# A fused pooling-mixer kernel: first operands in smaller pieces, weights in 4 KB rows, the second fold by passes, the first product by halves

## The chip, the cores and the metric

The kernel runs on one core of one Trainium2 chip. The metric is the device time of one execution in microseconds; of the kernel before there are three runs, 907.3, 907.58 and 908.1, and the profile of one execution.

## The reference, cut to what matters

With DEPTH = 1 only mixer 0 runs. `x` is 4096 frames by 1024 channels, all in float32:

```python
def pool_mixer(h, in_w, group_w, group_b, scale, out_w):
    u, gate = jnp.split(h @ in_w, 2, axis=-1)
    ug = u.reshape(b, s, POOL_GROUPS, POOL_GROUP_DIM)
    pooled = jnp.stack([trailing_mean(ug[:, :, g], w) for g, w in enumerate(POOL_WINDOWS)], axis=2) - ug
    mixed = jnp.einsum('bsgc,gcd->bsgd', pooled, group_w) + group_b
    y = mixed.reshape(b, s, POOL_WIDTH) * scale * jax.nn.silu(gate)
    return y @ out_w
...
    normed = rms_norm(h, norm_w[i])
    h = h + pool_mixer(normed, ...)
return rms_norm(h, final_norm_w)
```

The group map of each of the four groups (256 by 256) is linear and the pooling acts along frames alone, so the map can be multiplied into the first half of `in_w` ahead of time. The kernel does this itself at its start; it is called the fold.

## The kernel before, in words

**The whole.** After the fold, the input product is done for four blocks of 1024 frames, each as seven products of a Strassen-like scheme (P1 to P7, in the order P1, P2, P7, P6, P5, P4, P3); all four blocks go through it for the gate side (steps "a"), then through it for the folded side (steps "b"), and eight blocks of 512 frames go through the output product (steps "o"). A float32 product is made of three passes: each operand is split into a high part (rounded to the type that the profile shows as fp32r) and a low part (the rest), and high by high, high by low and low by high are added up in a PSUM bank (`mm3`, L814). Splitting is one copy on ScalarE for the high part and one subtraction on VectorE for the low part (`split`).

**The opening.** Only this part is touched. It runs from the start to about 50 us, and TensorE's work in it stands in this order:

1. eight matmuls on a constant (L1702) that need no data;
2. fold 1 and fold 2, in plain float32 (`fold`, L466): 8 matmuls each, which the trace shows as 16 records each;
3. fold 3 and fold 4 by passes, 24 matmuls each, on split operands;
4. fold 5, fold 6, fold 7 and fold 8 in plain float32 again, 16 records each; in the middle of fold 6 stand eight small matmuls (L532, `spread_rs`) that spread the first rows' normalization factors `hl` over the partitions;
5. the first product P1 of the first block (L814, 48 matmuls), then P2, in which eight more `spread_rs` matmuls stand behind the second group of six.

Each fold reads one block of `wut` (512 KB, the transposed first half of `in_w`) and a set of two group maps `gw` (512 KB; set 0 for folds 1 to 4, set 1 for folds 5 to 8). The blocks are numbered here like the folds that read them: block 1 is `ru[0, 0]`, block 2 `ru[0, 4]`, block 3 `ru[0, 2]`, block 4 `ru[0, 6]`, block 5 `ru[1, 0]`, block 6 `ru[1, 4]`, block 7 `ru[1, 2]`, block 8 `ru[1, 6]`. A fold writes two banks; ScalarE or VectorE carries them out with the norm weights as factors.

**What sets the order.** All loads of the opening but two are issued by the sync engine (SP) in program order, and they use eight semaphores in turn, so a load is issued when the load eight places before it has landed. The order on the queue is: set 0 and block 1 (1 MB in four transfers of 256 KB, one of them issued by ScalarE), blocks 2 to 4, three pieces of `x` rows, set 1, block 5, and so on. The gate weights `g0` (two loads of 512 KB out of `in_w`, for P1's weights) stand on either side of block 8. In HBM the group maps lie in rows of 1 KB for one partition, `wut` and the gate half of `in_w` in rows of 2 KB, `x` and `xt` in rows of 4 KB. VectorE, ScalarE and TensorE run their lists in the order that the tile scheduler gave them.

**P1.** `product_in` runs the 48 matmuls of P1 bank by bank (`by_bank`): for each of four banks first half 0 of the contraction, then half 1. Half h needs the operand `op` that is split from `xs[0]["11"][h]` and the weights `w[P1][h]`. Its four results are copied to other banks between its groups (`copy_first`).

Of the kernel before, what the change touches and what calls it, by code (L numbers as in the profile page):

```python
# [15 lines left out]
P = 128  # L16
D = 1024
S = 4096
H = 512
# [67 lines left out]
def kernel(  # L87
# [5 lines left out]
    wut: bass.AP,  # L93
    group_w: bass.AP,
    cols: bass.AP,
    inv_count: bass.AP,
# [327 lines left out]

    def load_group_w(q, halves=(0, 1), g=None):
        if g is None:
            g = take("p (t c) -> p t c", early, t=4)
        for j in halves:
            c = slice(2 * j, 2 * j + 2)
            sync.dma_start(  # L430
                out=g[:, c, :], in_=group_w[2 * q + j].rearrange("(t p) c -> p t c", p=P)
            )
        return g

    def load_wut(q, k, queues=(sync,)):
        r = take("p (k t c) -> p k t c", early5, k=2, t=4)
        by = 2 // len(queues)
        for n, queue in enumerate(queues):
            kk = slice(n * by, (n + 1) * by)
            queue.dma_start(  # L440
                out=r[:, kk],
                in_=wut[q, k + n * by : k + (n + 1) * by].rearrange("k p t c -> p k t c"),
            )
        return r

    def split_early(place, u, pattern, **sizes):

        flat = place.rearrange("p s a b -> p s (a b)")
        split(flat, u.rearrange("p a b -> p (a b)" if len(u.shape) == 3 else "p k t c -> p (k t c)"))
        return [flat[:, j].rearrange(pattern, **sizes) for j in range(2)]  # L450

    def fold(q, k, g, r, ps2, pool=None, on_vector=False, midway=None):
# [22 lines left out]
        o = take(pool=pool)  # L475
        for kk in range(2):
            if on_vector and kk == 0:
                with tc.issue_after(roots[0][1]):
                    vector.tensor_scalar(
                        out=o[:, kk], in0=ps2[kk], scalar1=norm_c[k + kk], scalar2=None,  # L480
                        op0=ALU.mult,
                    )
            else:
                dst, src = o[:, kk], ps2[kk]
                if by_passes:
                    dst = dst.rearrange("p (j s a) -> p j s a", j=2, s=2)
                    src = src.rearrange("p (j a s) -> p j s a", j=2, s=2)
                scalar.activation(dst, src, AF.Copy, scale=norm_c[k + kk])
# [1003 lines left out]
    def run(n, between=None, behind=None, seeds=4):  # L1492
# [4 lines left out]
        if kind == "o":  # L1497
            product_out(i, split_up.pop(n), sets, n == len(steps) - 1)
            evict_o(b, i, sets)
        else:  # L1500
            q = 0 if kind == "a" else 1
            if inner_in(q, b, i):
                us, parts = xs[b]["2"], []
                at["split"] += 1

                def next_half():
                    parts.append(split_half(us[len(parts)]))

                product_seven(split_up.pop(n), sets["v"], next_half, next_half)
                if b == NB - 1:  # L1510
                    give_kept(*places_in)
                split_up[n + 1] = parts
            else:
                product_in(i, split_up.pop(n), sets, i == P1, between, behind)
            if "second" in seven:
                seven.pop("second")()
            evict_in(b, q, i, sets, seeds)
            if "third" in seven:
                seven.pop("third")()
            if inner_in(q, b, i):  # L1520
                for u in xs[b].pop("2"):
                    give(u)
# [177 lines left out]
    warm = nc.const_aps.tensor(1.0, [P, H], mybir.dt.bfloat16)  # L1700
    for c in range(8):
        nc.tensor.matmul(  # L1702
# [10 lines left out]
    for j in range(3):  # L1713
        load_row(0, 0, j)
    gw[1] = load_group_w(1, (0,))
# [4 lines left out]
    load_group_w(1, (1,), gw[1])  # L1720
# [30 lines left out]
    for j in range(4):  # L1751
        load_row(0, 1, j, early if j < 3 else None)
    g1 = [load_rows(in_w, 4 + 2 * h, D) for h in range(2)]
    load(2)
    load(3)

    for h in range(2):
        sub(v0[h], v1[h], v0[h])
        copy(w[P7][h][:, 0], v0[h])

# [292 lines left out]
```

## Time and profile before

| | |
|---|---|
| runs | 907.3, 907.58, 908.1 us (median 907.58) |
| the profiled execution | span 905.6 us from first to last instruction; the median of the runs is 2.0 us more, which is what lies around a span |
| instructions | 12443 |
| TensorE busy | 895.4 us, 99% of the span |
| VectorE, ScalarE, GpSimd busy | 737.0, 519.2, 152.2 us |
| DMA | 209.60 MB, mean 231 GB/s |

How it is read: PE is TensorE's matmul, DVE VectorE, ACT ScalarE, POOL GpSimd, SP the sync engine; SPq and ACTq are their queues' issues. Matmuls are pipelined, so a record is longer than the distance to the next one: in a row of n merged records the share of one is the row's time over n. In the page's digit rows each digit is a busy share in tenths. In the issue rows the last number is the time from issue to landing.

### The profile page before, as it was taken

How to read it: one execution, taken by the hardware profiler on the slowest of the kernel's cores; microseconds unless marked ns; L12 is line 12 of the kernel's file. 1: busy time of each engine (PE TensorE's matmuls, PEld its weight loads, DVE VectorE, ACT ScalarE, POOL GpSimd, SP SyncE). 2: the span in 40 equal slices, each digit the busy share in tenths (PEclk: the TensorE clock that was granted, in tenths of full speed). 3: DMA queues.
4: the chain of work that ended last, by engine and by line, in shares of the span. 5: the costliest groups of instructions: out<-in, count | busy, mean ns of one | idle time of the engine just before them, and what ended most of it. 6: DMA issues, size and time to landing. Idle time of an engine off the chain costs nothing.

```text
span 905.6 us, 12443 instructions
## 1 busy us (share of the span) xinstructions
PE 895.4 (99%) x4554; PEld 792.2 (87%) x4554; DVE 737.0 (81%) x910; ACT 519.2 (57%) x848; POOL 152.2 (17%) x250
## 2 busy tenths in 40 slices
PE   9999999999999999999999999999999999999996
PEld 7888888888888888889889888988889899998995
DVE  3899896984996996995485499698898788888798
ACT  7869547446445467446345654744557466565464
POOL 0030110110111000010100011021233343342330
PEclk9999999999999999999999999999999999999999
DMA  9989778678769475854245386699573855945953
GB/s 342 401 316 322 260 279 320 215 296 284 269 251 369 171 260 203 313 195 170 90 140 185 140 302 232 233 330 306 152 213 81 221 171 150 238 149 131 266 176 116
DMA packets 78620, 209.60 MB, mean 231 GB/s; under 512 B 7392, under 2 KB 25184, under 8 KB 77792
## 3 DMA queue, kind: packets, MB, share of 16 engines
q1 hardware_dynamic: 57872, 143.77, 45.7%
q0 software_dynamic: 19968, 63.98, 22.7%
q10 hardware_dynamic: 720, 1.06, 0.3%
q8 instruction: 35, 0.57, 0.3%
q14 instruction: 25, 0.20, 0.1%
HBM read 133.28 MB, written 75.51 MB: 231 GB/s over the span
## 4 chain that ended last, share of the span: by engine, by line
PE 88%; DVE 5%; DMA 3%; ACT 2%; issue 2%; POOL 0%; DVEq 0%; ACTq 0%; POOLq 0%; SPq 0%
PE bank L814 76%; PE bank L956 5%; PE bank L760 3%; PE bank L466 3%; DVE vt L79 2%; DVE op L79 2%; DVE st L79 1%; DMA vt<-yd 1%; DMA st<-wvd 1%; ACT vt L79 1%; DMA early<-in_group_w 0%; ACT st L79 0%; ACT op L79 0%; DMA out<-vt 0%; DVE columns L79 0%
## 5 line engine op out<-in xcount | busy, mean ns | idle before, releaser
L814 PE MATMUL bank<-op,w 128*128 128x512 f32 x2544 | 551.2, 379 | 1.5 <-ACT st L79 1.0
L814 PEld LDWEIGHTS bank<-op,w 128*128 128x128 f32 x2544 | 480.2, 189 | 70.9 <-ACT st L79 1.8
L814 PE MATMUL bank<-w,op 128*128 128x512 f32 (+1 forms) x1044 | 230.5, 377 | 0.0
L814 PEld LDWEIGHTS bank<-w,op 128*128 128x128 f32 x1044 | 192.3, 189 | 25.0
L79 DVE TENSOR_TENSOR op<-st,op 128x1024 fp32r<-128x1024 f32 x119 | 144.9, 1223 | 55.7 <-ACT op L79 55.4
L79 ACT ACTIVATE op<-st 128x1024 fp32r<-128x1024 f32 x119 | 124.8, 1052 | 81.6 <-PE bank L814 32.3
L79 ACT ACTIVATE op<-vt 128x1024 fp32r<-128x1024 f32 x66 | 69.4, 1053 | 70.0 <-DVE vt L79 41.7
L79 DVE TENSOR_TENSOR op<-vt,op 128x1024 fp32r<-128x1024 f32 x66 | 79.8, 1222 | 22.2 <-ACT op L79 22.1
L79 ACT ACTIVATE vt<-bank 128x512 f32<-128x512 f32 (+1 forms) x124 | 68.7, 577 | 46.0 <-PE bank L814 38.3
L79 DVE TENSOR_TENSOR st<-st,st 128x1024 f32<-128x1024 f32 (+2 forms) x49 | 54.8, 1134 | 30.4 <-ACT st L79 16.7
L79 ACT ACTIVATE bank<-bank 128x512 f32<-128x512 f32 (+1 forms) x84 | 41.1, 489 | 51.4 <-PE bank L814 38.6
L79 POOL COPY vt<-tails 128x32 f32<-128x32 f32 x14 | 17.5, 1257 | 271.7 <-DVE inner L79 106.8
L79 DVE TENSOR_TENSOR vt<-bank,vt 128x512 f32<-128x512 f32 (+1 forms) x92 | 52.9, 603 | 6.2 <-PE bank L956 4.6
L79 ACT ACTIVATE st<-bank 128x512 f32<-128x512 f32 (+1 forms) x60 | 34.2, 586 | 35.6 <-PE bank L814 25.0
L79 ACT ACTIVATE st<-st 128x1024 f32<-128x1024 f32 (+1 forms) x37 | 38.9, 1056 | 21.7 <-DVE st L79 19.7
L79 DVE TENSOR_TENSOR st<-bank,st 128x512 f32<-128x512 f32 (+1 forms) x70 | 42.6, 627 | 4.7 <-PE bank L956 2.5
L79 POOL DMA_DIRECT2D sd<-st x45 | 24.0, 533 | 125.7 <-DVE st L79 77.7
L956 PEld LDWEIGHTS bank<-w,op 128*128 128x128 f32 x312 | 40.4, 191 | 1.7
L956 PE MATMUL bank<-w,op 128*128 128x256 f32 x312 | 41.1, 275 | 0.0
L79 DVE TENSOR_TENSOR st<-st,vt 128x1024 f32<-128x1024 f32 (+1 forms) x33 | 38.5, 1187 | 2.8 <-DMA vt<-rd 2.8
L79 DVE TENSOR_TENSOR_SCAN vt<-vt,window 128x1040 f32<-128x1040 f32 x16 | 38.0, 2381 | 0.1
L79 DVE TENSOR_TENSOR vt<-vt 128x1024 f32<-128x1024 f32 (+3 forms) x42 | 37.7, 899 | 0.1
(119 smaller groups left out, 770.3 us busy)
## 6 DMA issues: line engine op xcount, KB each, us to landing
sd<-st POOLq DMA_DIRECT2D x45, 512.0 KB, 4.7
st<-sd SPq DMA_DIRECT2D x43, 512.0 KB, 4.7
st<-in_xt SPq DMA_DIRECT2D x28, 512.0 KB, 7.6
st<-in_x SPq DMA_DIRECT2D x21, 512.0 KB, 7.7
yd<-st SPq DMA_DIRECT2D x19, 512.0 KB, 3.0
vt<-yd SPq DMA_DIRECT2D x17, 512.0 KB, 10.7
out<-vt POOLq DMA_DIRECT2D x16, 512.0 KB, 3.3
st<-yd SPq DMA_DIRECT2D x15, 512.0 KB, 8.0
```

The costliest lines, as they stand in the source:

```text
L79: r = f(*args, **kwargs)
L466: latest[0] = nc.tensor.matmul(ps, a[:, kk, 2 * j + t, :], maps, start=t + m == 0, stop=t == 1 and m == len(pairs) - 1,).ins
L760: latest[0] = nc.tensor.matmul(cell(n, c).rearrange("p (a s) -> p a s", s=2), x1, x2, start=i == P1 and k + m == 0, stop=k == 1 and m == 2 ...
L814: latest[0] = nc.tensor.matmul(ps, a, b, start=start and n == 0, stop=stop and n == 2, skip_group_check=True).ins
L956: latest[0] = nc.tensor.matmul(ps, x1, x2, start=start and k + n == 0, stop=k == 1 and n == 2, skip_group_check=True,).ins
```

## The change

- **First operands.** `load_first` takes the place of two loaders for set 0 and block 1. Set 0 comes as 128 KB, 128 KB and 256 KB; block 1 as 128 KB (issued by ScalarE), 128 KB and 256 KB. The constant matmuls go from eight to five.
- **Layout.** `group_w`, `wut` and the gate half of `in_w` (a new input `gate_w`) are laid out by the host so that a partition's share of a 512 KB load is one row of 4 KB.
- **Fold 2 by passes.** Set 0 is split ahead of fold 2 (before: ahead of fold 3), block 2 is split on VectorE alone (copy and subtraction), and fold 2 runs as 24 matmuls.
- **Order of loads.** Block 7 goes behind both loads of `xs[0]["11"]`; both gate loads go ahead of block 8.
- **P1 by halves.** The first P1 runs half 0 on all four banks, then half 1; three of its bank copies move from places 4, 6, 8 to 5, 6, 7 of its eight groups.
- **Two copies** of high parts of the first weights for P7 (`w[P7]`) move from ScalarE to VectorE.

```diff
+    def load_first():
+        g = take("p (t c) -> p t c", early, t=4)
+        r = take("p (k t c) -> p k t c", early5, k=2, t=4)
+        for t, queue in enumerate((scalar, sync)):
+            kt = slice(2 * t, 2 * t + 2)
+            sync.dma_start(out=g[:, t], in_=group_w[0, :, t])
+            queue.dma_start(out=r[:, 0, kt], in_=wut[0, 0, :, 0, kt])
+        sync.dma_start(out=g[:, 2:], in_=group_w[0, :, 2:])
+        sync.dma_start(out=r[:, 1], in_=wut[0, 0, :, 1])
+        return g, r
...
+        if on_vector:
+            vector.tensor_copy(out=flat[:, 0], in_=u)
+            sub(flat[:, 1], u, flat[:, 0].bitcast(F32))
+        else:
+            split(flat, u)
...
-                product_in(i, split_up.pop(n), sets, i == P1, between, behind)
+                product_in(i, split_up.pop(n), sets, i == P1 and n > 0, between, behind)
...
-    for c in range(8):
+    for c in range(5):
...
-    gw[0] = load_group_w(0)
-    ru[0, 0] = load_wut(0, 0, (scalar, sync))
+    gw[0], ru[0, 0] = load_first()
...
-    v1[0] = fold(0, 4, gw[0], ru[0, 4], pairs_of[1])
-    ru[1, 4] = load_wut(1, 4)
-
     maps = split_early(w[P6][0], gw[0], "p (t c) -> p t c", t=4)
     give(gw[0])
+    second = split_early(w[P7][0], ru[0, 4], "p (k t c) -> p k t c", True, k=2, t=4)
+    give(ru[0, 4])
+    v1[0] = fold(0, 4, maps, second, pairs_of[1], on_vector=True)
+    ru[1, 4] = load_wut(1, 4)
...
-            xs[0]["11"] = load_x(0, 0, 0, lambda: ru.update({(1, 2): load_wut(1, 2)}))
+            xs[0]["11"] = load_x(0, 0, 0)
+            ru[1, 2] = load_wut(1, 2)
     for hh in range(2):
-        if hh:
-            ru[1, 6] = load_wut(1, 6)
-        g0.append(load_rows(in_w, 2 * hh, D))
+        g0.append(load_gate(2 * hh))
+    ru[1, 6] = load_wut(1, 6)
...
-        copy(w[P7][h][:, 0], v0[h])
+        vector.tensor_copy(out=w[P7][h][:, 0], in_=v0[h])
...
-    run(0, {4: copy_first(0), 6: copy_first(1), 8: copy_first(2)}, seeds=3)
+    run(0, {5: copy_first(0), 6: copy_first(1), 7: copy_first(2)}, seeds=3)
```

Three places show how instructions move. The first is the start of SP's queue; `early_0_108` is set 0, `early_0_112` is block 1 and then block 2.

```order
-L79 DMA early_0_108<-in_group_w 128x2x256 x2
+L79 DMA early_0_108<-in_group_w 128x256 x2
+L79 DMA early_0_112<-in_wut 128x256
+L79 DMA early_0_108<-in_group_w 128x512
 L79 DMA early_0_112<-in_wut 128x512
-L79 DMA early_0_112<-in_wut 128x2x512
+L79 DMA early_0_112<-in_wut 128x1024
```

Two more issues stand ahead of block 2 (the row with 128x1024 for one partition), for the same number of bytes.

The second is VectorE's list at fold 2. `w_0_81` is the low part of set 0, `w_0_83` block 2, `w_0_79` and `w_1_80` blocks 3 and 4, `st_93<-bank_71` fold 2's first bank carried out.

```order
 L79 TENSOR_TENSOR w_0_81<-early_0_108,w_0_81 128x1024
+L79 CAST w_0_83<-early_0_112 128x1024
+L79 TENSOR_TENSOR w_0_83<-early_0_112,w_0_83 128x1024
 L79 TENSOR_TENSOR w_0_79<-early_1_113,w_0_79 128x1024
+L79 TENSOR_SCALAR st_93<-bank_71,colt 128x512
 L79 TENSOR_TENSOR w_1_80<-early_1_113,w_1_80 128x1024
```

The copy and the subtraction of block 2 stand ahead of the subtractions of blocks 3 and 4, and fold 2 waits for both.

The third is SP's queue further on. `early_1_113<-in_wut` is block 7 where it comes first and block 8 where it comes second, `st_94` and `st_95` are `xs[0]["11"]`, `st_96` and `st_97` the gate weights.

```order
 L79 DMA st_94<-in_xt 128x1024
-L79 DMA early_1_113<-in_wut 128x2x512
 L79 DMA st_95<-in_xt 128x1024
-L79 DMA st_96<-in_in_w 128x2x512
-L79 DMA early_1_113<-in_wut 128x2x512
-L79 DMA st_97<-in_in_w 128x2x512
+L79 DMA early_1_113<-in_wut 128x1024
+L79 DMA st_96<-in_gate_w 128x1024
+L79 DMA st_97<-in_gate_w 128x1024
+L79 DMA early_1_113<-in_wut 128x1024
 L79 DMA st_99<-in_xt 128x1024
```

Block 7 and block 8 each come one transfer later. Behind about 50 us the instructions of every engine stand in the order of before.

More of the change, by code (lines that the diff above doesn't have):

```diff
@@ L94 @@
     group_w: bass.AP,
+    gate_w: bass.AP,
     cols: bass.AP,
@@ L421, in plain, with load_group_w, load_wut, load_gate @@
         return bank.rearrange("p (a s) -> p s a", s=2)
[L425 to L432, printed above, removed]
+    def load_first():
[8 more added lines that the diff above has]
+        return g, r
+    def load_group_w(q):
+        g = take("p (t c) -> p t c", early, t=4)
+        sync.dma_start(out=g, in_=group_w[q])
         return g
-    def load_wut(q, k, queues=(sync,)):
+    def load_wut(q, k):
         r = take("p (k t c) -> p k t c", early5, k=2, t=4)
[L437 to L443, printed above, removed]
-        return r
-    def split_early(place, u, pattern, **sizes):
-        flat = place.rearrange("p s a b -> p s (a b)")
-        split(flat, u.rearrange("p a b -> p (a b)" if len(u.shape) == 3 else "p k t c -> p (k t c)"))
+        sync.dma_start(out=r, in_=wut[q, k // 2])
+        return r
+    def load_gate(k):
+        u = take()
+        sync.dma_start(out=u, in_=gate_w[k // 2])
+        return u
+    def split_early(place, u, pattern, on_vector=False, **sizes):
+        flat = place.rearrange("p s a b -> p s (a b)")
+        u = u.rearrange("p a b -> p (a b)" if len(u.shape) == 3 else "p k t c -> p (k t c)")
+        if on_vector:
[3 more added lines that the diff above has]
+            split(flat, u)
         return [flat[:, j].rearrange(pattern, **sizes) for j in range(2)]
@@ L476, in fold @@
         for kk in range(2):
+            dst, src = o[:, kk], ps2[kk]
+            if by_passes:
+                dst = dst.rearrange("p (j s a) -> p j s a", j=2, s=2)
+                src = src.rearrange("p (j a s) -> p j s a", j=2, s=2)
             if on_vector and kk == 0:
[L478 removed]
+                with tc.issue_after(roots[0][1]) if roots else nullcontext():
                     vector.tensor_scalar(
[L480 to L487 removed]
+                        out=dst, in0=src, scalar1=norm_c[k + kk], scalar2=None, op0=ALU.mult,
+                    )
+            else:
                 scalar.activation(dst, src, AF.Copy, scale=norm_c[k + kk])
@@ L1752 @@
         load_row(0, 1, j, early if j < 3 else None)
-    g1 = [load_rows(in_w, 4 + 2 * h, D) for h in range(2)]
+    g1 = [load_gate(4 + 2 * h) for h in range(2)]
     load(2)
@@ L2031 @@
         "group_w": group_w,
+        "gate_w": gate_w,
         "cols": cols,
```

8 lines of the change are left out of this document (4 added, 4 removed).

## The prediction, as put on record before the run

> **What bounds the kernel now.** I read the page first.
>
> ```profile
> span 905.6 us, 12443 instructions
> PE 895.4 (99%) x4554; PEld 792.2 (87%) x4554; DVE 737.0 (81%) x910; ACT 519.2 (57%) x848; POOL 152.2 (17%) x250
> PE 88%; DVE 5%; DMA 3%; ACT 2%; issue 2%; POOL 0%; DVEq 0%; ACTq 0%; POOLq 0%; SPq 0%
> ```
>
> TensorE is busy 99% of the span and has 88% of the chain that ended last: what it gains or loses in the opening it keeps, unless a later wait takes it. The view of waits, for TensorE, tells how few there are:
>
> ```profile
> PE bank L814 <- ACT st L79: 1.0, 2, 0.6
> PE bank L1702 <- PEq L2038: 0.8, 1, 0.8
> PE bank L814 <- DVE op L79: 0.5, 1, 0.5
> PE bank L466 <- DMA early<-in_group_w: 0.4, 1, 0.4
> ```
>
> Only the second and the last lie in the opening. The timeline of TensorE shows the opening as one unbroken row of work:
>
> ```profile
> 0.78 3.57 PE L1702 MATMUL bank<-const-bfloat16-1.0 128*128 128x512 bf16 x8 [0.78 <-PEq L2038]
> 4.72 7.54 PE L466 MATMUL bank<-early,early 128*128 128x256 f32 x32 [0.36 <-DMA early<-in_group_w]
> 11.91 5.71 PE L466 MATMUL bank<-w,w 128*128 128x256 f32 x48
> 17.45 5.35 PE L466 MATMUL bank<-early,early 128*128 128x256 f32 x24
> 22.45 1.29 PE L532 MATMUL bank<-w,hl 128*128 128x128 f32 x8
> 23.57 8.85 PE L466 MATMUL bank<-early,early 128*128 128x256 f32 x40
> 32.07 13.30 PE L814 MATMUL bank<-op,w 128*128 128x512 f32 x60
> 45.21 1.00 PE L532 MATMUL bank<-w,hl 128*128 128x128 f32 x8
> ```
>
> The rows are folds 1 and 2, 3 and 4, 5 with half of 6, the spread, the rest of 6 with 7 and 8, then P1. A plain fold's record takes 8.85/40 = 0.22 us, so a plain fold takes 3.5; a fold by passes takes 5.54/2 = 2.8. Fold 8 starts 24 records of 0.22 behind 23.57, at 28.75.
>
> But the DMA engines have no air either. The busy share of the DMA engines and GB/s in forty slices of the first 50 us:
>
> ```profile
> DMA  0299999999999999999999999999999999999941
> GB/s 0 33 346 385 285 375 375 415 418 406 385 374 382 396 379 405 392 401 388 388 387 400 405 408 410 413 410 393 393 400 398 411 410 403 393 406 416 387 177 43
> ```
>
> They are full from 2.5 us to 46. Loads land in the order of issue, so the opening has two clocks, TensorE's and the queue's, and the change must move both.
>
> **Part by part. First pieces.** Block 1's first half and the first quarter-megabyte of set 0 land together before TensorE's 4.72:
>
> ```profile
> early<-in_wut ACTq DMA_DIRECT2D x1, 256.0 KB, 3.6
> early<-in_group_w SPq DMA_DIRECT2D x1, 256.0 KB, 3.8
> ```
>
> Both were issued at 0.75, so they landed at 4.35 and 4.55. Now 256 KB less lies ahead of the first matmul; at 346 GB/s that is 0.76, so it starts at about 3.96. Five constant matmuls at 3.57/8 = 0.45 end near 3.0 and aren't in the way.
>
> ```profile
> 4.72 1.50 PE L466 MATMUL bank<-early,early 128*128 128x256 f32 x4 [0.36 <-DMA early<-in_group_w]
> ```
>
> These four records, with the pipeline's tail off, take about 1.34 instead of 0.88: the first ones still run at the rate of the constant matmuls, 0.45 a record, until about 5.6. Before, two records were done by then; now, from 3.96 at 0.45 each, nearly four. So fold 1 ends not 0.76 but 1.8 records earlier: 0.4, at 8.25 instead of 8.65. Set 0's rest and block 1's second half have the same bytes ahead of them as before and come in time.
>
> **Fold 2 by passes** saves 3.5 - 2.8 = 0.7 of TensorE, but adds a wait: block 2 must land, be copied and subtracted on VectorE, and TensorE's list behind it is in order.
>
> ```profile
> 2.24 0.43 SPq L79 DMA_DIRECT2D early<-in_wut  x1
> early<-in_wut SPq DMA_DIRECT2D x1, 512.0 KB, 5.9
> L79 DVE TENSOR_TENSOR w<-early,w 128x1024 fp32r<-128x1024 f32 x7 | 8.5, 1226 | 12.4 <-ACT w L79 12.4
> L79 DVE TENSOR_SCALAR early<-bank,colt 128x512 f32<-128x512 f32 x2 | 1.5, 749 | 0.0
> ```
>
> Block 2 landed at 2.24 + 5.9 = 8.1. The bytes ahead of it are the same, so I keep 8.1 (7.7 if the 285 GB/s slice just ahead, a third of a microsecond lost, doesn't come again). No row has VectorE copying 1024 elements from SBUF with one source: the rows bound it by 0.75 (half the elements, from a bank) and 1.23 (two sources, same elements); I take 1.2, the same shape in the same memory. Then the high parts are there at 9.4 and the low part at 10.6. The built order lets 4 of the 24 matmuls go on high parts of block 2; the other 20, at 0.115, end at 12.9. Before, fold 2 ended at 8.65 + 3.45 = 12.1. So the quarter that saves 0.7 of work ends **0.8 later**. At the lower bound it ends at 12.4, 0.3 later.
>
> [...]
>
> Folds 3 and 4 follow with no wait: block 3's subtraction comes behind block 2's, 10.6 + 1.2 = 11.8, and TensorE wants it at 12.9. VectorE's three copies (3.6 at 1.2) fall into the 12.4 us for which, by the row above, it idles ahead of these subtractions; without that cover the last of them, which stands ahead of `hl`, would hold the spread in fold 6 by 1.2.
>
> **Rows of 4 KB, and the order of loads.** A load on SP is issued when the one eight places ahead lands, so the distance of issues is that of landings:
>
> ```profile
> 20.36 0.34 SPq L79 DMA_DIRECT2D vt<-in_xt  x1
> 24.51 0.33 SPq L79 DMA_DIRECT2D early<-in_x  x1
> 25.83 0.33 SPq L79 DMA_DIRECT2D early<-in_x  x1
> 27.18 0.33 SPq L79 DMA_DIRECT2D vt<-in_x  x1
> 28.53 0.38 SPq L79 DMA_DIRECT2D vt<-in_in_w  x1
> 29.90 0.38 SPq L79 DMA_DIRECT2D vt<-in_in_w  x1
> 31.18 0.34 SPq L79 DMA_DIRECT2D vt<-in_xt  x1
> 17.54 0.38 SPq L79 DMA_DIRECT2D early<-in_wut  x1
> 18.82 0.37 SPq L79 DMA_DIRECT2D st<-in_in_w  x1
> early<-in_wut SPq DMA_DIRECT2D x1, 512.0 KB, 11.0
> st<-in_in_w SPq DMA_DIRECT2D x1, 512.0 KB, 11.1
> ```
>
> 24.51, 25.83, 27.18, 28.53 and 29.90 are the landings of block 7, `xs[0]["11"]`'s second half, gate 0, block 8 and gate 1 (block 8: 17.54 + 11.0, gate 1: 18.82 + 11.1). A load in 2 KB rows takes 1.35 to 1.37, one in 4 KB rows 1.28 (29.90 to 31.18): 0.08 each. Seven blocks and two gate loads make 0.65; set 1, before in 1 KB rows, at least 0.1: **0.7 in all by gate 1**. But block 8 now stands behind gate 1. It lands at 29.9 - 0.7 = 29.2 where it landed at 28.5, and fold 8 can start 0.15 behind that (as 4.72 behind 4.55), at 29.35 instead of 28.75: **0.6 later, however early TensorE comes**. Fold 2's 0.8 brings TensorE there at 29.55, with a copy of 0.75 at 29.05. Both ways give 0.6 to 0.8; block 7 (before at 24.5 for fold 7's 25.3, now at 25.8 less 0.5) costs at most 0.1 on the way and is in this. I take 0.7 at P1's start.
>
> ```profile
> 23.17 2.99 SPq L79 DMA_DIRECT2D early<-in_x  x3
> q8 instruction: 1, 0.02, 4.8%
> ```
>
> The gap from 20.36 to 23.17, where two landings are 2.8 apart instead of 1.3, goes with an instruction fetch on one of the DMA engines (the second row, of the stretch 20.5 to 21.9); all later landings carry that lag. Should it fall on an engine that is ahead, block 8 comes up to 1.0 earlier and only fold 2's lateness counts; kept as the lower end.
>
> **P1 by halves** had no wait to remove: the row at 32.07 follows without idle. It gives VectorE's weights for half 1 some 5 us more, which nothing needs: 0. In P2 the second spread (45.21) needs `hl`:
>
> ```profile
> 42.51 0.30 ACT L79 ACTIVATE tmp<-ss,eps 128x4 f32<-128x4 f32 x1
> 44.47 0.15 DVE L79 TENSOR_TENSOR hl<-rs,hl 128x4 fp32r<-128x4 f32 x1
> ```
>
> From the root's start to `hl`'s end it takes 2.1. Now bank 2's copy, which needs P1's 42nd matmul (33.0 + 42 x 0.22 = 42.1), stands ahead of the root on ScalarE together with a square of 1.2: root at 43.5 to 43.8, `hl` at 45.6 to 45.9, TensorE there at 45.9. 0 to 0.3; I take 0.
>
> **Sum:** 0.7 later: on the profiled execution's span 906.3, which with the 2.0 that the median of the runs has around it is 907.58 + 0.7 = **908.3**. Unknown ends: -0.3 (copy fast, lag small, block 2 early) to +1.3 (copy 1.2, block 8 as late as gate 1 was, `hl` late): 907.3 to 908.9.
>
> **Rivals.** *The queue isn't in the way* (0.22). If block 2 lands by 7, the copy is at the low bound and block 8 is there by 27.6, TensorE keeps its own gains: 0.4 + 0.7 = 1.1, so 906.5; with the whole 0.76 kept, 1.5, so 906.1. Against it: the full DMA row. For more than 1.8 something is needed that no term here has.
>
> *The small pieces starve the queue* (0.18, the slower side). SP's issues are 0.5 apart; 128 KB is 0.35 of transfer at 375 GB/s, and block 2's issue moves behind two more, from 2.24 to 3.2. If the engines run dry by s, everything behind is s later, block 8 lands at 29.2 + s, and the loss is 0.6 + s. It decides from s = 0.2, where the queue is later than fold 2, and at s = 1.2 gives 909.4. For it: issues slower than transfers. Against it: by 3.7 SP has issued 1.5 MB, and the engines, from 2.5 on at 375, have moved 0.45.
>
> *The slow rate lasts* (0.06). Full rate came at about 5.6, 4.8 behind the first constant matmul. Five of those end 1.3 earlier and leave TensorE idle for 0.9 ahead of fold 1. If the 4.8 then count from 3.96, full rate comes at 8.8, fold 1 ends at 9.9 and nothing is lost, since fold 2 waits for its split until 10.6 anyway; if they count twice, it comes at 13.6: fold 1 ends at 3.96 + 16 x 0.45 = 11.2, ten matmuls of fold 2 run at 0.23, fourteen at 0.115, and it ends at 15.1, 3.0 later than before: 910.6. [...]
>
> **How the numbers follow.** Forecast 0.54, queue not in the way 0.22, starving 0.18, slow rate 0.06. 0.2% is 1.8 us, about what a measurement of this kernel can tell from no change. Faster by more: 0.10, out of the first rival's unknown rest. Slower by more: two thirds of starving (0.12) and the slow rate, 0.18. Same: 0.72. The range, 906.0 to 910.0, takes in the first rival's worked times and most of starving; about 0.10 lies below and 0.09 above.
>
> **What would show it.** TensorE's first fold record near 3.9; idle ahead of fold 2 and within it, released by VectorE; fold 3's start 0.3 to 0.8 late; block 8 landing near 29.2 and fold 8 released by it; the same rows behind 50 us, shifted by a constant. It is wrong if fold 3 starts earlier than 11.9, if block 8 lands before 28.5, or if a new wait stands behind 50 us.

## The result, and the profile after

The changed kernel took **910.43 us** (median of 8 runs, 908.62 to 912.32), beside 907.84 for the kernel before (8 runs): a ratio of 1.0031, with a 95% interval of [1.0021, 1.0041]. It is slower, by about 2.6 us, and lies above the predicted range. The profiled execution has a span of 908.1 instead of 905.6.

Where the 2.5 of the span arose is seen in TensorE's timeline of the changed kernel (start, time, engine, line, shape and count; in brackets the idle time ahead and what ended it):

```profile
0.78 2.29 PE L1713 MATMUL bank<-const-bfloat16-1.0 128*128 128x512 bf16 x5 [0.78 <-PEq L2051]
4.19 2.08 PE L478 MATMUL bank<-early,early 128*128 128x256 f32 x4 [1.12 <-DMA early<-in_wut]
6.96 4.72 PE L478 MATMUL bank<-early,early 128*128 128x256 f32 x12 [0.69 <-DMA early<-in_group_w]
11.34 8.74 PE L478 MATMUL bank<-w,w 128*128 128x256 f32 x72
19.91 5.35 PE L478 MATMUL bank<-early,early 128*128 128x256 f32 x24
24.90 1.19 PE L543 MATMUL bank<-w,hl 128*128 128x128 f32 x8
25.93 8.85 PE L478 MATMUL bank<-early,early 128*128 128x256 f32 x40
34.43 13.30 PE L825 MATMUL bank<-op,w 128*128 128x512 f32 x60
47.57 1.01 PE L543 MATMUL bank<-w,hl 128*128 128x128 f32 x8
```

Fold 5 starts at 19.91 instead of 17.45, P1 at 34.43 instead of 32.07, the second spread at 47.57 instead of 45.21: 2.46, 2.36 and 2.36 later. All of the loss stands ahead of fold 5, and inside it ahead of 11.34, where fold 1 ends (before: about 8.65). Fold 1 starts half a microsecond earlier and ends 2.7 later, for two reasons that the rows show side by side. It waits: 1.12 ahead of its first record and 0.69 between its fourth and fifth. And it is slow: twelve records take 4.72, 0.39 each, where a plain record at full rate takes 0.22.

The chain of work that ended last, of the changed kernel's first 22 us (start, time, what), names what was waited for:

```profile
1.66 0.42 SPq L79
2.08 0.04 issue
2.12 4.70 DMA early<-in_group_w
6.83 0.14 issue
6.96 4.74 PE bank L478 x12
```

Set 0's last quarter-megabyte was issued by SP at 2.12, as its fourth load, and landed at 6.83. In the kernel before the same bytes were issued at 1.23 and landed at 5.55. The view of DMA issues (KB each, time from issue to landing) has for the kernel before, of set 0's and of block 1's second half:

```profile
early<-in_group_w SPq DMA_DIRECT2D x1, 256.0 KB, 4.3
early<-in_wut SPq DMA_DIRECT2D x1, 256.0 KB, 4.3
```

and for the changed kernel, of block 2 and of the same two:

```profile
early<-in_wut SPq DMA_DIRECT2D x1, 512.0 KB, 6.7
early<-in_group_w SPq DMA_DIRECT2D x1, 256.0 KB, 4.7
early<-in_wut SPq DMA_DIRECT2D x1, 256.0 KB, 5.9
```

Block 1's second half, issued at 2.60, landed at 8.5 (before: 1.74 + 4.3 = 6.0), block 2, issued at 3.07, at 9.8 (before: 8.1). So the queue was not only issued later, it moved less. GB/s in forty slices of the stretch from 3 to 9 us, of the kernel before:

```profile
GB/s 389 396 382 362 376 389 376 368 361 350 438 361 403 410 410 314 205 205 232 259 287 341 355 341 410 437 410 369 355 328 300 328 369 396 382 423 410 396 410 396
```

and of the changed kernel:

```profile
GB/s 315 280 354 320 312 339 252 264 262 314 307 287 219 191 246 178 191 218 246 246 191 300 328 328 341 369 232 219 300 246 273 341 328 396 369 437 382 410 437 437
```

Before has one dip of half a microsecond (205 to 259, near 5.5); the changed kernel stays mostly at 180 to 340 from 4 to 8. In that stretch 37 packets of 2 and 4 KB took 0.2 to 1.1 us each (18 in the kernel before); the usual one of 2 KB takes 0.084 in both kernels.

The slow rate goes with TensorE's granted clock: in the changed kernel with eight constants (below) 10 records in 3.41 us stand beside a granted clock of 0.50. There the clock's changes lie 3.41 apart, so the stretches here have that length. Two of them in the kernel before (length, PE busy time and records, granted clock, DMA share, GB/s; ahead of the first recorded change, 5.53 here and 10.80 in the changed kernel, the clock column reads 1.00 also where the records are slow, so the records are counted instead):

```profile
2.12:5.53 3.41, 3.05 (x8) 1.00 1.01 327
5.53:8.94 3.41, 3.41 (x17) 1.00 0.98 353
```

and in the changed kernel (here with weight loads, DVE, ACT and POOL between PE and the clock):

```profile
0.56:3.97 3.41, 2.29 (x5) 0.59 (x5) 0.12 (x2) 1.49 (x2) 0.00 (x0) 1.00 0.50 140
3.97:7.39 3.42, 2.50 (x5) 1.64 (x6) 0.00 (x0) 0.46 (x1) 0.00 (x0) 1.00 0.92 262
7.39:10.80 3.41, 3.41 (x9) 2.61 (x9) 2.17 (x3) 1.48 (x4) 0.00 (x0) 1.00 1.00 391
10.80:14.21 3.41, 3.41 (x29) 3.30 (x29) 1.79 (x2) 2.49 (x3) 0.00 (x0) 1.00 1.02 411
```

In the kernel before, full rate begins at 5.53: 17 records in the stretch behind it. In the changed kernel the stretch from 7.39, though as full of work, has 9: half rate lasts until 10.80. The stretches ahead of it have 1.1 and 0.9 of idle time; before's last slow one had 0.36.

Theories at this point. **Late pieces**: the small first pieces make the first megabyte and a half land 1.3 to 2.5 late, whatever TensorE does. **Slow clock**: TensorE's idle time, made by five constants instead of eight and by the waits inside fold 1, keeps the half rate. **The split**: fold 2's wait for block 2's copy and subtraction, which the prediction had as its largest term.

### The profile page after: what moved, and what is told of

Its sections match the earlier page's. It is cut to its first block, busy times and chain, and to the rows that moved or that the text cites. A ratio compares the mean times of both kernels' runs of the same rounds, so it can differ in the third digit from the quotient of the medians.

```text
span 908.1 us, 12466 instructions
## 1 busy us (share of the span) xinstructions
PE 896.6 (99%) x4559; PEld 792.8 (87%) x4559; DVE 741.1 (82%) x915; ACT 516.9 (57%) x845; POOL 152.0 (17%) x250
## 4 chain that ended last, share of the span: by engine, by line
PE 94%; DVE 3%; ACT 1%; DMA 1%; issue 1%; SPq 0%; DVEq 0%; ACTq 0%
PE bank L825 82%; PE bank L967 6%; PE bank L771 3%; PE bank L478 3%; DVE vt L79 1%; DVE st L79 1%; ACT vt L79 1%; DMA early<-in_group_w 1%; DMA vt<-in_x 0%; DVE op L79 0%; ACT st L79 0%; DVE columns L79 0%; PE bank L543 0%; DVE w L79 0%; SPq L79 0%
```

## The experiments

All ratios are to the kernel before, run on the same chip beside it (its median there 907.6 to 907.7), with 11 runs of each version (5 of the contiguous one) and 21 to 33 of the kernel before. The clock, the landings and the timelines of a version are those of its one profiled execution.

### Each half of the first operands' change alone

**Eight constants** in the changed kernel:

```diff
-    for c in range(5):
+    for c in range(8):
```

> The changed kernel with eight constant matmuls again instead of five; all else as changed. Theory A, late pieces: the first megabyte and a half lands late (set 0's last quarter-megabyte pair at 6.8, block 1's second half at 8.5, block 2 at 9.8), whatever TensorE does ahead. Full rate then comes near 5.5 as before, but fold 1 still waits for 8.5 and ends at 8.6 + 8 x 0.22 = 10.4, and fold 2 waits for block 2's split (9.8 + 0.7 + 1.2 = 11.7) and ends near 14.0: fold 5 starts at 19.6 instead of 19.9, the time is 0.3 less than the changed kernel's 910.4: 910.1. Theory B, slow rate: TensorE's idle time behind five constants keeps it at half rate until 10.8; with eight the rate is full from 5.5 and most of the 2.5 lost comes back: 908.2. Theory C, split of block 2: as A, with the idle time now seen ahead of fold 2.

909.33 us, ratio 1.0018 [1.0009, 1.0026]. About 1.1 comes back by the medians, more than late pieces alone allow and less than the slow clock alone; the interval overlaps that of the changed kernel, so the 1.1 is rough. The profiled execution shows the clock's changes; the first recorded one lies at 4.29:

```profile
0.88:4.29 3.41, 3.41 (x9) 1.12 (x9) 0.06 (x1) 1.49 (x2) 0.00 (x0) 1.00 0.61 180
4.29:7.71 3.42, 1.46 (x7) 1.00 (x7) 0.00 (x0) 0.47 (x1) 0.00 (x0) 1.00 0.74 241
7.71:11.12 3.41, 3.41 (x10) 2.71 (x9) 2.76 (x3) 1.46 (x4) 0.00 (x0) 0.50 1.02 408
```

The first stretch, without idle time, was followed by full clock (1.00 from 4.29); in that one TensorE waited 1.97 for set 0's rest, and the next was granted 0.50; that one had no idle time, and full clock came again (1.00, 29 records). The changes lie at 4.29, 7.71 and 11.12, 3.41 apart. In this execution 1.97 of idle time in 3.42 was followed by half the clock.

**Pieces of 256 KB** in the changed kernel, with its five constants:

```diff
-        for t, queue in enumerate((scalar, sync)):
-            kt = slice(2 * t, 2 * t + 2)
-            sync.dma_start(out=g[:, t], in_=group_w[0, :, t])
-            queue.dma_start(out=r[:, 0, kt], in_=wut[0, 0, :, 0, kt])
+        sync.dma_start(out=g[:, :2], in_=group_w[0, :, :2])
+        scalar.dma_start(out=r[:, 0], in_=wut[0, 0, :, 0])
```

> The changed kernel with set 0 and block 1 in four transfers of 256 KB as before (still rows of 4 KB in HBM, five constants, fold 2 by passes). Theory A, late pieces: block 2 lands at 8.1 again, block 1 by 6.0; fold 2 ends near 11.5 to 12.2 and fold 5 starts near 17.4: 2.2 to 2.5 less, 908.0 to 908.3. Theory B, slow rate from the idle time behind five constants: the idle time grows (3.0 to 4.6), so half rate lasts to about 11 again; fold 1 ends at 4.7 + 16 x 0.43 = 11.5 and nothing comes back: 910.4 or a little more.

909.3, 1.0019 [1.001, 1.0028]: between the two again. The landings came back as expected (block 2 at 7.4); fold 1 then started at 4.54 behind 1.46 idle, and its 16 records took 5.54 (3.72 with eight constants beside the same pieces, below).

**Five constants in the kernel before**, and nothing else:

```diff
-    for c in range(8):
+    for c in range(5):
```

> The kernel before with five constant matmuls instead of eight and nothing else. Theory D, windows of 3.41 with half rate behind one with much idle time: TensorE idles from 3.1 to 4.5, full rate comes at 7 to 10 instead of 5.5, fold 1 ends up to 2 later; nothing takes it back: 1.0 to 1.9 more than before, 908.7 to 909.5. Theory of the prediction's likeliest case, that full rate comes a fixed time after the start of work: no difference, 907.6.

909.02, 1.0011 [1.0002, 1.002]. TensorE's timeline of it has the wait and its price:

```profile
0.78 2.29 PE L1702 MATMUL bank<-const-bfloat16-1.0 128*128 128x512 bf16 x5 [0.78 <-PEq L2038]
4.65 9.75 PE L466 MATMUL bank<-early,early 128*128 128x256 f32 x32 [1.57 <-DMA early<-in_group_w]
14.05 5.71 PE L466 MATMUL bank<-w,w 128*128 128x256 f32 x48
```

Folds 1 and 2 take 9.75 instead of 7.54 in this execution; by the medians three constant matmuls that compute nothing are worth 1.4 (the interval reaches from 0.2 to 1.8).

**Both undone**: pieces of 256 KB and eight constants, all else as changed (fold 2 by passes, layout, order of loads, P1 by halves).

> The changed kernel with both at once: set 0 and block 1 in four transfers of 256 KB, and eight constant matmuls; fold 2 by passes, layout and the rest as changed. The two runs before it showed each alone giving back about half. Theory D, windows: the granted clock is set in windows of 3.41, and a window in which TensorE idled is followed by one at half rate; here no window has more than 0.4 idle, so full rate comes by 5.5, fold 1 ends at 8.4, fold 2 (split ready at 7.5 + 0.7 + 1.2 = 9.4) ends at 11.7, fold 5 starts at 17.3: 907.5, no different from before. Rival, the split of block 2 costs beside that: fold 5 at 18 or later, 908.3. Rival, half rate is a matter of the time since the start and not of idle time: half until 8 to 11 and 909.3 as with five constants.

907.44, 1.0002 [0.9993, 1.0011]: no difference from before. Late pieces and slow clock together are the whole loss, as far as an interval of 0.8 us to either side can tell. Its timeline of TensorE shows what is left of the split's wait:

```profile
4.63 3.72 PE L476 MATMUL bank<-early,early 128*128 128x256 f32 x16 [0.55 <-DMA early<-in_wut]
8.46 0.68 PE L476 MATMUL bank<-w,w 128*128 128x256 f32 x4
9.63 7.86 PE L476 MATMUL bank<-w,w 128*128 128x256 f32 x68 [0.49 <-DVE w L79]
17.33 5.61 PE L476 MATMUL bank<-early,early 128*128 128x256 f32 x24
```

Fold 2 begins on the high part, waits 0.49 for the low part, and fold 5 starts at 17.33 (before: 17.45).

### Fold 2 and the layout

**Fold 2 plain** in the changed kernel, with set 0's split behind it:

```diff
+    v1[0] = fold(0, 4, gw[0], ru[0, 4], pairs_of[1])
+    ru[1, 4] = load_wut(1, 4)
...
-    second = split_early(w[P7][0], ru[0, 4], "p (k t c) -> p k t c", True, k=2, t=4)
-    give(ru[0, 4])
-    v1[0] = fold(0, 4, maps, second, pairs_of[1], on_vector=True)
-    ru[1, 4] = load_wut(1, 4)
```

> The changed kernel with fold 2 in plain float32 as before (set 0 split behind it, block 2 not split). Theories A and B: fold 2 follows fold 1 at once in the changed kernel already, so the plain fold only costs its longer work, 3.5 instead of 2.8, less the 0.25 that fold 3 waited: 0.4 more, 910.8. Theory C, the wait for the split is what costs: 0.8 less, 909.6.

909.48, 1.0021 [1.0012, 1.003]. The median is near the 909.6 that was expected if the wait for the split is what costs. But the interval overlaps that of the changed kernel, the executions of the two scatter over 2.9 and 3.7, and in the profiled one fold 5 starts at 21.13, 1.2 later than in the changed kernel and not earlier. So this run alone tells little. The same edit with pieces of 256 KB and eight constants does better:

> As the kernel with 256 KB pieces and eight constants, but fold 2 plain: what is left of the change is the layout, the order of loads, P1 by halves and two copies moved. Theory D: fold 1 and 2 as before, fold 3 at 11.8, fold 5 at 17.3: 907.5, and the difference from the kernel with fold 2 by passes (its wait for the split, against its shorter work) is within 0.3. If the moved loads hold fold 8 (block 8 behind gate 1): fold 8 released by a DMA and 0.3 to 0.6 more.

907.25, 1.0001 [0.9992, 1.0011], beside 1.0002 with fold 2 by passes. Fold 5 starts at 17.28 and 17.33, with fold 1 at full rate in both (the 32 records of folds 1 and 2 take 7.17 in the first, the 16 of fold 1 3.72 in the second, 0.22 and 0.23 each). Fold 2 by passes neither gains nor costs by more than can be told; and block 8, which lands at 28.2 behind both gate loads, does not hold fold 8 (28.5).

**The layout alone**, on the kernel before (loads from rows of 4 KB, in the old order and pieces):

```diff
-                out=g[:, c, :], in_=group_w[2 * q + j].rearrange("(t p) c -> p t c", p=P)
+                out=g[:, c, :], in_=group_w[q, :, c]
...
-                in_=wut[q, k + n * by : k + (n + 1) * by].rearrange("k p t c -> p k t c"),
+                in_=wut[q, k // 2, :, kk],
...
-        g0.append(load_rows(in_w, 2 * hh, D))
+        g0.append(load_gate(2 * hh))
```

> The kernel before with only the layout changed: set 0 and 1, the blocks and the gate weights in rows of 4 KB, in the old order, pieces, constants and with fold 2 plain. By the prediction's step on rows each load takes 0.08 less, gate 1 lands 0.7 earlier (29.2 instead of 29.9) and block 8 at 27.9 instead of 28.5, but TensorE waits for none of them: 907.8, within 0.3 of before. A rival, that halves of 4 KB rows are themselves slow to read at the start: block 2 later than 8.5 and up to 0.5 more, 908.3.

907.49, 0.9999 [0.999, 1.0008]. Gate 1 landed at 28.2 instead of 29.9 and nothing waited for it. Block 2 landed at 7.6 instead of 8.1.

### Why the pieces are late

**Contiguous pieces.** The four loads of 128 KB read 1 KB out of every 4 KB row. Here each is one contiguous piece of HBM (a new input; the same transfers otherwise):

```diff
-            sync.dma_start(out=g[:, t], in_=group_w[0, :, t])
-            queue.dma_start(out=r[:, 0, kt], in_=wut[0, 0, :, 0, kt])
+            sync.dma_start(out=g[:, t], in_=first_w[0, t])
+            queue.dma_start(
+                out=r[:, 0, kt], in_=first_w[1, t].rearrange("p (t c) -> p t c", t=2)
+            )
```

> The changed kernel with the four pieces of 128 KB each contiguous in HBM, instead of 1 KB out of every 4 KB row; the same transfers in number, size and order, five constants. Theory A1, reading 1 KB out of 4 KB rows is what makes the pieces and those behind them late: set 0's rest lands by 5.6 (6.8 in the changed kernel), block 1's second half by 6.2 (8.5), block 2 by 8.1 (9.8); some half rate is left from the idle time behind five constants: 909.0 to 909.4. Theory A2, the number of small transfers is what makes them late: the landings stay and so does the time, 910.4.

910.89, 1.0038 [1.0026, 1.0051]. The first two pieces landed 0.6 earlier (3.4 and 3.6) and set 0's rest at 7.1, block 1's second half at 7.8, block 2 at 9.3: still late; that is 0.3 later than in the changed kernel for the first, and 0.5 to 0.7 earlier for the other two. The way the rows are read is at most a small part of the cause.

**Issues moved, twice.** First, in the changed kernel with eight constants, ScalarE issues both small pieces of block 1 (`scalar` in place of `queue` in the loop). That takes one issue off SP's list:

> The changed kernel with eight constants, and both 128 KB pieces of block 1 issued by ScalarE instead of one: everything behind them is issued one place (0.47) earlier on SP. Theory A2a, the pieces behind are late because each small transfer takes an issue's place on SP: set 0's rest, block 1's second half and block 2 land 0.5 earlier than with eight constants alone (7.1, 7.8, 9.2), and the time is 0.3 to 0.5 less than its 909.3. Theory A2b, the small transfers themselves, wherever issued, make the DMA engines slow: landings as with eight constants alone, 909.3.

907.8, 0.9998 [0.9989, 1.0007]: no difference from before that can be told, a microsecond less than either theory had. Set 0's rest landed at 6.05, block 1's second half at 7.5, block 2 at 8.7. Fold 1's first eight records took 3.08, its last eight 1.99, and the 68 of folds 2 to 4 behind the wait for the split 7.86, as with pieces of 256 KB: full rate came within fold 1 and held. In the profiled execution P1 still starts at 32.95, 0.9 later than before, though the span is only 0.2 longer: a wait of TensorE at 223 us, 0.43 of idle time in the profiled execution of the kernel before, is missing in this one, so there part of the opening's loss was taken back.

Second, the kernel with 256 KB pieces and eight constants gets two more loads of 4 KB, used by nothing, in SP's list:

```diff
+        for n in range(2):
+            sync.dma_start(out=extra[n], in_=eye[:, 0:8])
         sync.dma_start(out=g[:, 2:], in_=group_w[0, :, 2:])
```

> The kernel with 256 KB pieces and eight constants (907.4), with two loads of 4 KB that nothing needs ahead of set 0's second half: SP's issues of it, of block 1's second half and of block 2 come at 2.1, 2.6 and 3.1, as in the changed kernel, but without small pieces of the operands. Theory A2a, issue pace: block 2 lands at 8.5 to 9.8 instead of 7.4, 908.4 or more. Theory A2b, the small transfers of operands: landings within 0.3 of those without the two loads, 907.4 to 907.7.

908.6, 1.0009 [0.9999, 1.0019]. By the time it is at the edge of what can be told; by the landings it is not. Block 2, of the view of issues without the two loads and with them:

```profile
early<-in_wut SPq DMA_DIRECT2D x1, 512.0 KB, 5.2
```

```profile
early<-in_wut SPq DMA_DIRECT2D x1, 512.0 KB, 6.1
```

It is issued at 2.12 and 3.07, and lands at 7.3 and 9.2: 8 KB more in the queue (256 packets of 32 bytes) and 0.95 in the issue cost 1.9 in the landing. From 5.1 to 6.15 the DMA engines of the kernel with these loads moved 41 to 205 GB/s.

**The same two loads issued by ScalarE**, off SP's list:

> The kernel with 256 KB pieces, eight constants and two more 4 KB loads, these now issued by ScalarE instead of SP: SP issues set 0's second half, block 1's second half and block 2 at 1.2, 1.65 and 2.1 as without them. Theory A2a, the pace of issues on SP: block 1's second half lands near 6.0 and block 2 at 7.3 to 7.6 as without the two loads; 907.4 to 907.7. Theory A2b, the small transfers in the queues: block 1's second half at 7.5 to 8, block 2 at 8.5 to 9.2 as with the loads on SP; 908.3 to 908.6.

The landings are those of theory A2a. Block 2, issued at 2.13:

```profile
early<-in_wut SPq DMA_DIRECT2D x1, 512.0 KB, 5.4
```

It lands at 7.5, and block 1's second half at 6.2: as without the two loads. The time, 908.33, is the one that theory A2b had, but at 1.0004 [0.9995, 1.0013] it is no difference from before that can be told. Blocks 3 and 4 were now issued late, at 4.8 and 5.2 instead of 2.6 and 3.1, and block 4 landed at 11.1 instead of 10.1: block 3's issue came right behind the landing of block 1's first half, at 4.80, as loads take eight semaphores in turn and two more of them bring that turn forward.

**All small pieces, three issued by each of the two engines**, and eight constants, so that SP issues block 2 at 2.12:

> The changed kernel with eight constants and all its small pieces, but block 1's three pieces issued by ScalarE and set 0's three by SP, so that SP issues block 2 at 2.1 as before and not at 3.1. Theory A2a, the pace of issues: set 0's rest by 5.5, block 1's second half by 6.2, block 2 at 7.4 to 7.7; fold 1 starts at 4.15, has little idle time, fold 2 waits for its split (7.5 + 0.7 + 1.2 = 9.4) and ends at 11.7, fold 5 at 17.3: 907.3, no different from before, since the split and not fold 1 sets the end. Theory A2b, the small transfers: block 1's second half at 7.5 or later, block 2 at 8.7 or later and 907.8 to 909.3.

908.37, 1.0005 [0.9996, 1.0014]. Block 2 landed at 8.05, 0.7 later than with pieces of 256 KB, and 1.2 to 1.7 earlier than in the changed kernel and in that with eight constants. So the issue's place, or what else leaves SP's queue with it, is the larger part, and the small pieces themselves a smaller one.

**Four transfers, two of them small** (128 KB, then 384 KB, of each operand), and eight constants:

```diff
+        sync.dma_start(out=g[:, 0], in_=group_w[0, :, 0])
+        scalar.dma_start(out=r[:, 0, 0:2], in_=wut[0, 0, :, 0, 0:2])
+        sync.dma_start(out=g[:, 1:], in_=group_w[0, :, 1:])
+        sync.dma_start(
+            out=flat[:, 256:], in_=wut[0, 0].rearrange("p k t c -> p (k t c)")[:, 256:]
+        )
```

> The changed kernel with eight constants, and set 0 and block 1 each in pieces of 128 KB and 384 KB: four transfers as before, the first two of them small. Theory A2 in either form, the number of small transfers: landings of block 1's end near 6.1 and of block 2 near 7.5 again; the first two matmul records start at 4.1 and the next ones wait for 384 KB of set 0 (near 5.5), an idle time of 0.6 to 0.9 and with it some half rate: 907.8 to 908.8. Rival, any piece of 128 KB ahead slows what follows: block 2 at 9 or later and 909.3.

907.66, 1.0 [0.9991, 1.0009]. Fold 1 starts at 4.22, as early as in the changed kernel, block 2 lands at 7.5, and the full rate holds (fold 1's last twelve records take 2.86, in the changed kernel 4.72). Even so nothing is won on before: fold 5 starts at 17.34. It is the best that the idea gave, and no version that ran is faster than the kernel before by more than its interval.

| Kernel | SP issues block 2 | it lands | us | ratio |
|---|---|---|---|---|
| 256 KB, eight constants | 2.12 | 7.3 | 907.44 | 1.0002 |
| 128 and 384 KB, eight constants | 2.12 | 7.5 | 907.66 | 1.0 |
| 256 KB and two loads by ScalarE | 2.13 | 7.5 | 908.33 | 1.0004 |
| small pieces, half by ScalarE | 2.12 | 8.05 | 908.37 | 1.0005 |
| small pieces, one more by ScalarE | 2.60 | 8.7 | 907.8 | 0.9998 |
| 256 KB and two loads by SP | 3.07 | 9.2 | 908.6 | 1.0009 |
| small pieces, eight constants | 3.07 | 9.2 | 909.33 | 1.0018 |
| changed (small pieces, five constants) | 3.07 | 9.8 | 910.43 | 1.0031 |

The landings follow the issue, and other executions bear it out: in three more versions with 256 KB pieces in 4 KB rows block 2, issued at 2.12, lands at 7.4 to 7.6, and in three more with small pieces, issued at 3.07, at 9.0 to 9.3. The times of the first six rows follow neither: they lie within 1.2 us of each other, and each interval reaches 0.8 or 0.9 to either side.

One rival is left. Every version with the late issue has more transfers in SP's own queue, and every one with the issue back in place has fewer there, since they were left out or went to ScalarE's queue. No run delays the issue alone, so the moment of the issue and what stands in SP's queue ahead of it are not told apart.

### The clock taken out, the late pieces left

The changed kernel with eight constants, and eight more between fold 1's second and third matmul, where it waits:

```diff
+                if first and (kk, j) == (0, 1):
+                    for c in range(8):
+                        nc.tensor.matmul(
+                            banks[4 + c % 4], warm[:, 0:P], warm,
+                            start=True, stop=True, skip_group_check=True,
+                        )
```

> The changed kernel with eight constants at the start and eight more constant matmuls (their results are used by nothing) between fold 1's second and third matmul, where TensorE waited 2.0 for set 0's rest; small pieces as changed. Theory D, windows: TensorE has no window with much idle time, so full rate lasts from 4 to 5.5 on; fold 1 waits for block 1's second half (7.8 to 8.5) and ends at 9.6 to 10.3, fold 2 waits for its split and ends at 13.5: 0.9 to 1.0 less than with eight constants alone (909.3), 908.4. What stays above before (1 or so) is the late pieces' share. If idle time has no part in it: no less than 909.3, and more if the fillers run at half rate (8 x 0.43 = 3.4 instead of 1.7).

909.14, 1.0018 [1.0009, 1.0027]: no less than with eight constants alone, so the expected 0.9 did not come in the median. What came is evenness: 908.49 to 909.85, where eight constants alone gave 908.26 to 911.57. In the profiled execution the eight constants inside fold 1, from 5.87, took 1.91 (those at the start 3.57) and the twelve records behind them 2.75, so full rate held there, and fold 5 started at 19.25, still 1.8 late. That fits idle time inside fold 1 that costs the clock with eight constants in some executions and not in the middle one (the profiled one, which lost it, took 910.25); but the clock of the others is on record only as a mean over the whole run, so this is not shown. With the full rate held, the late pieces alone are worth about 1.5.

## Why the prediction was wrong

It said 908.3 with 906.0 to 910.0; the time is 910.43. The step that failed is the one on the first pieces: "Set 0's rest and block 1's second half have the same bytes ahead of them as before and come in time". They landed at 6.83 and 8.51 instead of 5.55 and 6.01. Bytes ahead were the same, issues ahead were two more, and by the runs with issues moved that is the larger part of the lateness. With it fell "the first ones still run at the rate of the constant matmuls, 0.45 a record, until about 5.6": the half rate lasted to 10.80 in the profiled execution. Fold 1, set at 8.25, ended at 11.3. The sum of 0.7 had nothing for either; measured apart, the late pieces are worth about 1.5 (909.14, with the rate held) and the three missing constants 1.4 (909.02).

Point by point:

- *Start of fold 1*: 3.96 predicted, 4.19 measured. The 0.23 is that the last small piece of the pair landed at 4.15.
- *Five constants "aren't in the way"*: true of their end (3.07), not of the idle time behind it. In the kernel before the cut alone cost 1.4 by the medians; on top of the small pieces it cost 1.1 (910.43 against 909.33, with intervals that overlap).
- *Fold 2's split, 0.8 later*: the sign that was named for it, idle time ahead of fold 2 and in it, did not come: from 11.34 the changed kernel has 72 records without a break, since fold 1 ended so late that the split was no longer waited for. In the kernel with 256 KB pieces and eight constants the mechanism was there, but not the size. The copy took 0.69 (predicted 1.2, with 0.75 as the lower bound), and with the pieces in time block 2 lands at 7.3 to 7.5, not 8.1 (the layout alone brings 7.6). VectorE's rows of the kernel with 256 KB pieces and eight constants:

```profile
7.63 0.69 DVE L79 CAST w<-early 128x1024 fp32r<-128x1024 f32 x1
8.35 1.23 DVE L79 TENSOR_TENSOR w<-early,w 128x1024 fp32r<-128x1024 f32 x1
```

  The split ends at 9.6, and fold 5 starts at 17.33, with plain fold 2 at 17.28: the term is about nothing.
- *Rows of 4 KB, 0.7 by gate 1*: right: gate 1 came 1.7 earlier in the layout's run, of which 1.0 is a smaller lag of one DMA engine (the last of sixteen ends 0.59 behind the fifteenth, in the kernel before 1.60), and 0.7 is left. *Block 8 at 29.2, fold 8 0.6 later*: it landed at 29.20 in the changed kernel, by luck: one DMA engine lagged 0.17 behind the other fifteen there, and 1.59 in the kernel before, which made up for loads that came 1.4 late. Nobody waited, since TensorE came to fold 8 at 31.1. With the pieces in time it lands at 28.2 to 28.5, about when it is wanted.
- *P1 by halves, 0, and the second spread, 0 to 0.3*: right. From P1's start to the second spread it is 13.14 in both kernels.
- *A constant shift behind 50 us*: 2.4 until a wait at 223 us, 0.43 of idle time in the profiled execution of the kernel before, which the changed one has not; 1.8 to 2.3 from there to the end.

Of the rivals, "the small pieces starve the queue" had the place and the sign, at a chance of 0.18. The reason given against it, that SP has issued 1.5 MB by 3.7 and the engines have moved less, was read wrongly: with those bytes issued the engines moved mostly 180 to 340 GB/s from 4 to 8 us. So was "the full DMA row": from 3.97 to 7.39 the changed kernel's DMA engines count as busy for 0.92 and moved 262 GB/s, from 7.39 on for 1.00 and 391. Here the busy share did not tell the bytes. "The slow rate lasts", at 0.06, was right too: half rate lasted to 10.80. The prediction weighed it only with a count from the first matmul, not with the idle time of each stretch (0.92 ahead of the slow one from 7.39 to 10.80, 0.36 in the kernel before ahead of full rate). The two together, not one, made the 2.6, and the forecast had no case in which both came.

What stays open: why a queue whose transfers are issued a microsecond later moves mostly 180 to 340 GB/s for some microseconds, with packets of 0.2 to 1.1 us, while it has over half a megabyte issued ahead. The runs show that it comes and goes with the place of the issues on SP and that contiguous reads do not cure it; what takes the time in these packets no view shows.

## What to carry to other kernels

At a kernel's start count issues, not bytes: here every load cost its place (0.47 us on SP) in the list of the engine that issues it, and a turn of the semaphores, and what came behind paid more than that place (block 2 landed 1.9 later for 0.95 of issue). Smaller first pieces stopped costing time here when the number of loads ahead of the next operand stayed the same, or another engine issued them; even then they won nothing. Keep TensorE busy until its operands land: in the changed kernel a stretch with 0.92 of idle time was followed by 3.41 us with 9 records where the kernel before has 17, so matmuls on a constant that are "not in the way" should not be cut by their end, but by the idle time that they leave.

## What was not expected of the hardware

Half the clock did not follow on the same amount of idle time in every execution (stretches of 3.41 us as above, counted back from the first recorded change where they lie ahead of it). Of those at half rate, one with 0.36 idle (the kernel before, 2.12 to 5.53) was followed by full rate, 17 records in 3.41 us; those with 0.92 (the changed kernel, 3.97 to 7.39) and 1.55 (five constants in the kernel before, 3.10 to 6.51) were followed by 9 and 10 records. With contiguous pieces 0.55 of idle time ahead of fold 1 and 1.56 behind its fourth record went with twelve records in 5.46, as slow. Of those at full rate, the one with 1.97 idle (eight constants) was followed by 0.50, the one with 1.25 was not: in the kernel with two more loads by SP the eight constants end early, at 3.94 instead of 4.35, so full rate was there from about 3.39, and the two stretches behind are

```profile
3.39:6.81 3.42, 2.17 (x9) 1.19 (x8) 0.00 (x0) 0.44 (x1) 0.00 (x0) 1.00 1.05 277
6.81:10.22 3.41, 2.79 (x13) 1.83 (x12) 2.17 (x3) 1.70 (x5) 0.00 (x0) 1.00 0.96 366
```

with the clock at 1.00 in both, though TensorE idled for 1.25 of the first; eight records behind it, from 7.95, took 1.99. In this same kernel the 3.39 us ahead of the first of these have 0.78 idle and were followed by full rate as well. All of it lies ahead of the first matmul, and whether that time counts no run shows. From which amount of idle time the clock falls these few executions do not tell.

The first recorded change to full rate lies at 5.53, 10.80 and 4.29 in three profiled executions (the kernel before, the changed one, and that with eight constants). Counted back in steps of 3.41, the distance of the changes in the last of them, that gives 2.12, 0.57 and 0.88: no one time from the kernel's start. That idle time in the opening makes executions scatter more is not shown: the changed kernel's 8 runs span 3.7 us, but the kernel before spans 1.9 to 3.4 in its sets of 8 to 33 runs (leaving out one run of 5441.6 us), and with five constants it spans 1.8 in 11.
